# A feed-forward product as seven block products instead of eight, with its activations kept in DRAM

## The chip, the cores and the metric

The kernel runs on one core of a Trainium2 chip. The metric is the device time of one execution in microseconds (us); less is better. Before the change three runs gave 2440.69, 2441.7 and 2443.47 us, median 2441.7.

## The reference

One layer of a streaming encoder on 1024 tokens of 1024 channels, all float32. Four token mixers feed four gated branches that are merged and projected; what the change touches comes behind that:

```python
x = layer_norm(ALPHA * x + merged @ w_out[l], ln1_g[l], ln1_b[l])
ff = jnp.square(jax.nn.relu(x @ w_ff1[l])) @ w_ff2[l]          # 1024 -> 4096 -> 1024
ple = (p[l] @ w_ple[l]) * jax.nn.sigmoid(x @ w_ple_gate[l] + b_ple_gate[l])
x = layer_norm(ALPHA * x + ff + ple, ln2_g[l], ln2_b[l])
```

`p` has 256 channels. `ALPHA` is 2 to the power 1/4.

## The kernel before, in words

Every product of float32 operands is made from float32r parts: `Gemm.split` (L346) lets ScalarE copy a tile into its high part and VectorE subtract that to get the low part, and `Gemm.acc` (L362) issues three matmuls for each pair of 128x128 weights and 128x512 data: high by high (L367), high by low (L368), low by high (L369). `Gemm.load` (L350) brings a weight tile (512 KB for 1024 columns) into one of two buffers `wf` and splits it by halves into `wh` and `wl`, of which there are three each.

The program has four stretches: the mixers, attention along with the gates, the branches with the output projection `wo` and the first norm, and the feed-forward with the embedding. A scheduling layer sets the order on each engine from its own costs; within an engine instructions run in that order. Only the last stretch (L910 to L1072) changes.

- `norm` (L926) gives token-major tiles `x1[i]` of 128 tokens. `x1_transposed` (L948) turns a tile by eight TensorE transposes into PSUM (`tx`); ScalarE writes the high part `x1H` from there (L960) and VectorE the low part `x1L` (L961), channel-major.
- `feed_forward` (L1028) takes two of the 32 tiles of 128 hidden channels at a time (the last call four). For each tile and each half of the tokens (512) it needs 8 x 3 = 24 matmuls over the 1024 input channels (L1038), then relu on ScalarE (L1040), the square on GpSimd (L1041) and a split into `ah`, `al` in SBUF (L1042). The second product (L1057) follows at once: 16 half tiles of 128 tokens by 512 channels, 6 matmuls each (12 in the last call), added into `x1` by VectorE (L1061). The weights `w2f` are split at L1050.
- `embedding` (L991) runs twice, for 512 output channels each, token-major: 8 x 24 matmuls for the gate (`pg`, L1018), 8 x 6 for `p @ w_ple` (`pl`, L1024), then VectorE, ScalarE (tanh) and GpSimd (the sum into `x1`, L1026).
- The last call of `feed_forward` runs the second norm after each tile of tokens and stores it.

All DMAs are issued from SyncE's queue, in its order. `tmp` gives one of four 128x512 buffers; `pst` (L987) goes round all eight PSUM banks.

Of the kernel before, what the change touches and what calls it, by code (L numbers as in the profile page):

```python
# [45 lines left out]
class Rwkv:  # L46
    """RWKV-7 in chunks of 64 tokens; a unit is two chunks (128 tokens) of four heads.

    With D the decay accumulated within a chunk, at = -kk D[t-1], rt = r D[t], bt = kk a / D, kt = k / D, for kk
    before its normalisation, and g = 1 / |kk|^2 (token by token, on a diagonal):  # L50
    S = g (I - Aab g)^-1 (at P + Aak V), o = rt P + Qrb S + Qrk V, P' = D[end] (P + bt^T S + kt^T V).
    b and k are stacked on the partitions, (b|k) in a unit's first chunk and (k|b) in its second.
    """
# [34 lines left out]
    def unit(s, hf, b):  # L88
# [173 lines left out]
        # ---- the chunks in sequence  # L262
# [27 lines left out]
        # ---- group norm, bonus, gate  # L290
# [42 lines left out]
NG = 14        # gate tiles computed ahead, along with the recurrence  # L333
NH = 8         # gate tiles computed ahead, along with the attention
NA = 1.6       # attention steps traced per half tile of products around them


class Gemm:
    """Products of float32 operands, each split exactly into two float32r parts."""
# [10 lines left out]
    def load(s, dram, n, name, whole=False):  # L350
        """the k-tiles of a weight tile: [(hi, lo)]"""
# [21 lines left out]
def trunk(ctx, tc, xT, xn, pT, w_in, w_gate, w_branch, w_out, w_ff1, w_ff2, w_ple, w_pg,  # L373
          pvd, mud, bgd, lrud, lora, biasd, b256, rows, cstd, mskd, out):
# [48 lines left out]
    with tc.tile_pool(name="mx", bufs=1) as mx:  # L423
# [7 lines left out]
        for _ in range(NZ):   # the array's clock rises with use  # L431
            T.matmul(pz, wz[:, 0:128], wz, start=True, stop=True)
# [715 lines left out]
```

## Time and profile before

| what | value |
|---|---|
| median of three runs | 2441.7 us |
| span of the profiled execution | 2437.5 us, that is 4.2 us less than the median |
| TensorE busy | 2405.2 us, 99% |
| VectorE busy | 1217.1 us, 50% |
| ScalarE busy | 772.2 us, 32% |
| GpSimd busy | 222.5 us, 9% |
| memory traffic | 199.29 MB, mean 82 GB/s |
| stretch of the change | from about 1616 us, the end of `wo`, to the end |

The span is what the profile shows of one execution, and its own time isn't listed apart from it; the 4.2 us to the median stand for what lies around it. In the profile a matmul's duration covers its way through the array, and the next begins before it ends, so durations of matmuls overlap.

### The profile page before, as it was taken

What the parts mean: (1) busy time and instruction counts of PE and PEld (TensorE: products, weight loads), DVE (VectorE), ACT (ScalarE), POOL (GpSimd) and SP (SyncE); (2) the same over time, 40 slices, a digit from 0 to 9 for tenths busy, and PEclk for the clock granted to TensorE, in tenths of its full rate; (3) what the DMA queues carried; (4) which work ended last, traced back from release to release, by engine and by line L of the source; (5) the groups of instructions that cost most, each with busy time, mean ns of one, the idle gap of its engine ahead of it and who ended that gap; (6) DMA issues with size and microseconds to landing.
All of it is one profiled execution on the core that took longest, in us unless ns stands there. A gap on an engine that the chain in (4) does not pass through costs nothing.

```text
span 2437.5 us, 31399 instructions
## 1 busy us (share of the span) xinstructions
PE 2405.2 (99%) x12290; PEld 1984.6 (81%) x12290; DVE 1217.1 (50%) x2615; ACT 772.2 (32%) x1392; POOL 222.5 (9%) x238
## 2 busy tenths in 40 slices
PE   9999999999999999999999999999999999999998
PEld 7888787877777788878888887878888888888887
DVE  5354545767767542254534335664433434334337
ACT  5543323433424222243434343231212122121220
POOL 0000100010000100002111000001111010010111
PEclk9999999999999999999999999999999999999999
DMA  5531222121121112344412225321211111111112
GB/s 198 201 114 70 87 73 66 59 65 55 55 70 52 63 68 76 124 159 133 128 63 70 87 74 179 123 89 44 67 44 52 52 44 61 35 52 53 44 42 79
DMA packets 114563, 199.29 MB, mean 82 GB/s; under 512 B 18544, under 2 KB 53488, under 8 KB 114416
## 3 DMA queue, kind: packets, MB, share of 16 engines
q1 hardware_dynamic: 114416, 197.30, 24.6%
q8 instruction: 96, 1.57, 0.3%
q14 instruction: 51, 0.42, 0.1%
HBM read 154.27 MB, written 42.99 MB: 81 GB/s over the span
## 4 chain that ended last, share of the span: by engine, by line
PE 93%; DMA 2%; DVE 2%; ACT 1%; issue 1%; SPq 0%; POOL 0%; DVEq 0%; ACTq 0%; POOLq 0%
PE f L367 9%; PE f L369 9%; PE f L368 9%; PE ggt L368 4%; PE ggt L369 4%; PE ggt L367 4%; PE br L367 2%; PE br L369 2%; PE br L368 2%; PE gc L367 2%; PE gc L369 2%; PE gc L368 2%; PE gd L367 2%; PE gd L368 2%; PE po L785 2%; PE gd L369 2%
## 5 line engine op out<-in xcount | busy, mean ns | idle before, releaser
L369 PE MATMUL ggt<-xh,wlgt 128*128 128x512 f32 x512 | 202.5, 396 | 0.0
L367 PE MATMUL ggt<-xh,whgt 128*128 128x512 f32 x512 | 202.4, 395 | 0.0
L368 PE MATMUL ggt<-xl,whgt 128*128 128x512 f32 x512 | 202.1, 395 | 0.0
L367 PE MATMUL f<-w2h,ah 128*128 128x512 f32 x512 | 199.3, 389 | 0.9 <-ACT ah L347 0.9
L367 PE MATMUL f<-x1H,whf 128*128 128x512 f32 x512 | 199.3, 390 | 0.6 <-ACT x1H L960 0.6
L368 PE MATMUL f<-w2l,ah 128*128 128x512 f32 x512 | 199.2, 389 | 0.0
L368 PE MATMUL f<-x1L,whf 128*128 128x512 f32 x512 | 199.1, 389 | 0.0
L369 PE MATMUL f<-x1H,wlf 128*128 128x512 f32 x512 | 198.9, 389 | 0.0
L369 PE MATMUL f<-w2h,al 128*128 128x512 f32 x512 | 196.1, 389 | 0.0
L1061 DVE TENSOR_TENSOR x<-x,f 128x512 f32<-128x512 f32 x224 | 148.4, 685 | 73.3 <-PE f L369 72.6
L348 DVE TENSOR_TENSOR al<-rl,ah 128x512 fp32r<-128x512 f32 x64 | 44.2, 691 | 181.4 <-ACT ah L347 181.4
L1040 ACT ACTIVATE rl<-f 128x512 f32<-128x512 f32 x64 | 37.8, 591 | 272.5 <-PE f L369 272.5
L1041 POOL TENSOR_TENSOR rl<-rl 128x512 f32<-128x512 f32 x64 | 68.7, 1073 | 543.4 <-ACT rl L1040 543.4
L367 PEld LDWEIGHTS f<-w2h,ah 128*128 128x128 f32 x512 | 96.1, 188 | 21.1 <-ACT ah L347 1.2
L367 PEld LDWEIGHTS f<-x1H,whf 128*128 128x128 f32 x512 | 96.1, 188 | 20.8 <-ACT x1H L960 0.9
L368 PEld LDWEIGHTS f<-w2l,ah 128*128 128x128 f32 x512 | 96.1, 188 | 19.9
L369 PEld LDWEIGHTS f<-w2h,al 128*128 128x128 f32 x512 | 96.1, 188 | 20.0
L369 PEld LDWEIGHTS f<-x1H,wlf 128*128 128x128 f32 x512 | 96.1, 188 | 20.0
L368 PEld LDWEIGHTS f<-x1L,whf 128*128 128x128 f32 x512 | 96.1, 188 | 19.9
L369 PEld LDWEIGHTS ggt<-xh,wlgt 128*128 128x128 f32 x512 | 96.3, 188 | 19.1 <-issue 0.5
L368 PEld LDWEIGHTS ggt<-xl,whgt 128*128 128x128 f32 x512 | 96.3, 188 | 19.0 <-issue 0.3
L367 PEld LDWEIGHTS ggt<-xh,whgt 128*128 128x128 f32 x512 | 96.2, 188 | 18.3
(350 smaller groups left out, 5340.9 us busy)
## 6 DMA issues: line engine op xcount, KB each, us to landing
wfgt<-w_gate SPq DMA_DIRECT2D x32, 512.0 KB, 3.3
wff<-w_ff SPq DMA_DIRECT2D x32, 512.0 KB, 3.3
w2f<-w_ff SPq DMA_DIRECT2D x32, 512.0 KB, 3.3
gsd<-tg SPq DMA_DIRECT2D x44, 256.0 KB, 2.0
tl<-gsd SPq DMA_DIRECT2D x44, 256.0 KB, 3.1
zt<-zs SPq DMA_DIRECT2D x16, 640.0 KB, 5.0
qk<-qkv SPq DMA_DIRECT2D x64, 128.0 KB, 2.8
wfwb<-w_branch SPq DMA_DIRECT2D x32, 256.0 KB, 2.8
```

Source lines behind the costliest of these rows:

```text
L348: s.nc.vector.tensor_tensor(lo, src, hi.bitcast(F32), op=ALU.subtract)
L367: mm(ps, lh, rh, start=first and i == 0, stop=False)
L368: mm(ps, lh, rl, start=False, stop=False)
L369: mm(ps, ll, rh, start=False, stop=last and i == n - 1)
L785: T.matmul(po[:, 0:64], PT[:, c * 128:c * 128 + 128], vt[:, (k0 + c) * 128 + par * 64:(k0 + c) * 128 + par * 64 + 64], start=c == 0, stop= ...
L1040: A.activation(t, p, AF.Relu)
L1041: G.tensor_tensor(t, t, t, op=ALU.mult)
L1061: V.tensor_tensor(x1[i][:, sl], x1[i][:, sl], p, op=ALU.add)
```

## The change

The first feed-forward product and the embedding's gate product are computed in blocks of two by two: the weights of two hidden tiles by two halves of the input channels (a11, a12, a21, a22), the data by halves of the channels and of the tokens (blocks 11, 12, 21, 22). In place of eight block products of 12 matmuls, seven are made (Strassen's scheme in Winograd's form), from sums and differences of blocks.

- `combine` makes the sums of the data once, before the embedding: T1 = 12 - 11, T2 = 22 - T1, T3 = 22 - 12, T4 = 21 - T2, and splits 11, 21, T1, T2, T3, 22 and T4 into high and low parts. That is 28 splits of 128x512 and 16 subtractions of that size, those for T1 and T2 on VectorE, those for T3 and T4 on GpSimd. `x1_transposed` now only copies (`x1R`).
- `seven` does one pair of weight tiles: GpSimd makes S1 = a21 + a22, S2 = S1 - a11, S3 = a11 - a21 and S4 = a12 - S2, the last two in place in the `wf` buffers; each of the seven weight blocks is split, and the products accumulate in three PSUM banks a, b, c that are read between products.
- The embedding runs channel-major, four calls of `seven` (`pg0` to `pg3`), its bias now per partition in the tanh; each of its 16 results is turned back to tokens by four TensorE transposes (`pq`) and added to `x1` by four VectorE instructions of 128x128.
- All 16 calls of `seven` for the first product (`f10` to `f115`) come before the second product. Activations go to a DRAM tile `actd` as float32, 64 stores of 256 KB, and come back as 32 loads of 512 KB in `feed2`, where VectorE and ScalarE split them (`a2h`, `a2l`). The second product's matmuls are as before.

Its core:

```diff
+        def seven(w0, w1, name, sink, tiles=htmp):
+            wf = []
+            for i, w in enumerate((w0, w1)):
+                t = wp.tile([128, 1024], F32, tag="wf", name=f"wf{name}{i}", bufs=2)
+                SY.dma_start(t, w)
+                wf.append(t)
+            a11, a12, a21, a22 = (t[:, h * 512:h * 512 + 512] for t in wf for h in range(2))
+            def product(src, n, p, x, first=True):
+                wh = wp.tile([128, 512], F32R, tag="wh", name=f"wh{name}{n}")
+                wl = wp.tile([128, 512], F32R, tag="wl", name=f"wl{name}{n}")
+                gm.split(src, wh, wl)
+                gm.acc(p, [(wh[:, k * 128:k * 128 + 128], wl[:, k * 128:k * 128 + 128]) + XB[x, k] for k in range(4)], first, skip_group_check=not first)
...
+            a = ps("g", f"a{name}")
+            product(a11, 1, a, "11")
+            p1 = tiles(f"p1{name}")
+            A.activation(p1, a, AF.Copy)
+            c = ps(f"r{ns[0] % 2}", f"c{name}")
+            product(a12, 2, c, "21")
+            V.tensor_tensor(p1, c, p1, op=ALU.add)
+            sink(0, 0, p1, None)
+            yield
+            s1 = total(1, a21, a22, ALU.add)
+            s2 = total(2, s1, a11, ALU.subtract)
+            product(s2, 3, a, "T2", first=False)
+            u2 = tiles(f"u2{name}")
+            A.activation(u2, a, AF.Copy)
+            b = ps("q", f"b{name}")
+            product(s1, 4, b, "T1")
+            p5 = tiles(f"p5{name}")
+            A.activation(p5, b, AF.Copy)
+            s3, s4 = a21, a12
+            G.tensor_tensor(s3, a11, a21, op=ALU.subtract)
+            G.tensor_tensor(s4, a12, s2, op=ALU.subtract)
+            product(s3, 5, a, "T3", first=False)
+            V.tensor_tensor(p5, a, p5, op=ALU.add)
+            sink(1, 1, p5, None)
+            product(s4, 6, b, "22", False)
+            V.tensor_tensor(u2, b, u2, op=ALU.add)
+            sink(0, 1, u2, None)
+            product(a22, 7, a, "T4", False)
+            sink(1, 0, None, a)
...
+                p3 = ps("s", f"pq{ct}{j}")
+                for q in range(4):
+                    T.transpose(p3[:, q * 128:q * 128 + 128], t[:, q * 128:q * 128 + 128], ident)
+                for q in range(4):
+                    xs_ = x1[4 * j + q][:, ct * 128:ct * 128 + 128]
+                    V.scalar_tensor_tensor(xs_, xs_, ALPHA, p3[:, q * 128:q * 128 + 128], op0=ALU.mult, op1=ALU.add)
...
+        def feed1(n):
+            def sink(i, j, t, p):
+                if t is None:
+                    t = htmp(f"rl{n}{i}{j}")
+                A.activation(t, t if p is None else p, AF.Relu)
+                G.tensor_tensor(t, t, t, op=ALU.mult)
+                SY.dma_start(actd[2 * n + i, :, j * 512:j * 512 + 512], t)
...
+        def feed2(n, fs, last=False):
             act, w2 = [], []
+            for f in fs:
+                for src, dst, nm in ((actd[f], act, "a"), (w_ff2[f], w2, "w")):
+                    wf = wp.tile([128, 1024], F32, tag="wf", name=f"{nm}2f{f}", bufs=2)
+                    SY.dma_start(wf, src)
+                    hi, lo = place(f"{nm}2h{f}"), place(f"{nm}2l{f}")
+                    gm.split(wf, hi, lo)
+                    dst.append((hi, lo))
```

How the order moves, at three places. First VectorE, between the last transposes of `x1` (`tx70`, `tx71`) and the first block products. Before, its rows there were short low parts of `x1`, straight from PSUM, and the first feed-forward weights and activations:

```order
L939 SCALAR_TENSOR_TENSOR x1_7_14317<-xr70_14260,mvn17_14319,b1_13687 128x512
L939 SCALAR_TENSOR_TENSOR x1_7_14317<-xr71_14289,mvn17_14319,b1_13687 128x512
L961 TENSOR_TENSOR x1L31_14352<-tx41_14342,x1H31_14351 128x2x128
L961 TENSOR_TENSOR x1L21_14348<-tx51_14364,x1H21_14347 128x2x128
L961 TENSOR_TENSOR x1L11_14339<-tx50_14355,x1H11_14338 128x2x128
L348 TENSOR_TENSOR pg00_14697<-pgf00_14695,pg00_14697 128x512
L348 TENSOR_TENSOR pg10_14700<-pgf00_14695,pg10_14700 128x512
L961 TENSOR_TENSOR x1L01_14335<-tx60_14373,x1H01_14334 128x2x128
```

Now, behind the copies of the last two transposes, stand the sums and splits of all blocks (`xT2l0` is the low part of T2):

```order
L971 TENSOR_SCALAR x1R01_14330<-tx70_14371 128x2x128
L971 TENSOR_SCALAR x1R21_14339<-tx71_14378 128x2x128
L1026 TENSOR_TENSOR x1R00_14048<-x1R01_14330,x1R00_14048 128x512 x2
L1026 TENSOR_TENSOR x1R10_14050<-x1R11_14332,x1R10_14050 128x512 x2
L1031 TENSOR_TENSOR xT20_14401<-x1R21_14339,x1R00_14048 128x512
L348 TENSOR_TENSOR x22l0_14448<-x1R21_14339,x22h0_14447 128x512
L1031 TENSOR_TENSOR xT20_14401<-x1R21_14339,x1R00_14048 128x512
L348 TENSOR_TENSOR x22l0_14448<-x1R21_14339,x22h0_14447 128x512
L1031 TENSOR_TENSOR xT21_14410<-x1R31_14341,x1R10_14050 128x512
L348 TENSOR_TENSOR x22l2_14454<-x1R31_14341,x22h2_14453 128x512
L1031 TENSOR_TENSOR xT21_14410<-x1R31_14341,x1R10_14050 128x512
```

From the copy of `tx71` to the split of the seventh weight block (`wlpg07`) VectorE has 32 such full-width rows, one of 1024 columns and one TENSOR_SCALAR.

Second, GpSimd in the middle of the first product. Before, it had only the squares:

```order
L1041 TENSOR_TENSOR rl150_17296<-rl150_17296 128x512
L1041 TENSOR_TENSOR rl151_17326<-rl151_17326 128x512
L1041 TENSOR_TENSOR rl160_17508<-rl160_17508 128x512
L1041 TENSOR_TENSOR rl161_17538<-rl161_17538 128x512
L1041 TENSOR_TENSOR rl170_17580<-rl170_17580 128x512
```

Now the sums of the next pair of weights stand between the squares of this one (`f19` is one call of `seven`, `f110` the next):

```order
L1142 TENSOR_TENSOR p1f19_16695<-p1f19_16695 128x512
L1074 TENSOR_TENSOR S1f110_16865<-wff1101_16823 128x512
L1142 TENSOR_TENSOR p5f19_16757<-p5f19_16757 128x512
L1074 TENSOR_TENSOR S2f110_16867<-S1f110_16865,wff1100_16821 128x512
L1097 TENSOR_TENSOR wff1101_16823<-wff1100_16821,wff1101_16823 128x512
L1142 TENSOR_TENSOR u2f19_16738<-u2f19_16738 128x512
L1098 TENSOR_TENSOR wff1100_16821<-wff1100_16821,S2f110_16867 128x512
L1142 TENSOR_TENSOR rl910_16817<-rl910_16817 128x512
```

There are eight instructions of GpSimd for each call, four of them sums that the next call's weight blocks wait for.

Third, VectorE at the begin of the second product, which now stands by itself:

```order
L348 TENSOR_TENSOR a2l4_18014<-a2f4_18011,a2h4_18013 128x1024
L1183 TENSOR_TENSOR x1_7_14313<-x1_7_14313,f2070_17843 128x512
L348 TENSOR_TENSOR w2l4_18020<-w2f4_18017,w2h4_18019 128x1024
L1183 TENSOR_TENSOR x1_7_14313<-x1_7_14313,f2071_17851 128x512
L1183 TENSOR_TENSOR x1_0_13751<-x1_0_13751,f2100_17883 128x512
L1183 TENSOR_TENSOR x1_0_13751<-x1_0_13751,f2101_17891 128x512
L348 TENSOR_TENSOR a2l5_18026<-a2f5_18023,a2h5_18025 128x1024
L1183 TENSOR_TENSOR x1_1_13821<-x1_1_13821,f2110_17899 128x512
```

Splits of loads that are needed a group later stand between the sums that free the PSUM banks (`f2070` and so on). On TensorE everything up to the output projection stands in the old order.

## Rows read from the trace of the kernel before

**Rows 1.** The page, busy time by engine: us, share of the span, instructions.
```profile
span 2437.5 us, 31399 instructions
...
PE 2405.2 (99%) x12290; PEld 1984.6 (81%) x12290; DVE 1217.1 (50%) x2615; ACT 772.2 (32%) x1392; POOL 222.5 (9%) x238
```

**Rows 2.** The page, costliest groups: count, busy us, mean ns, idle before.
```profile
L369 PE MATMUL f<-x1H,wlf 128*128 128x512 f32 x512 | 198.9, 389 | 0.0
```

**Rows 3.** Timeline of TensorE in the feed-forward: start, us; 19 rows of matmuls between.
```profile
1900.33 0.39 PE L367 MATMUL f<-w2h,ah 128*128 128x512 f32 x1
...
1904.86 0.39 PE L369 MATMUL f<-w2h,al 128*128 128x512 f32 x1
```

**Rows 4.** Windows: length, busy us of PE, PEld, DVE, ACT, POOL; PE clock, DMA.
```profile
1620.00:1630.00 10.00, 7.60 (x40) 5.62 (x39) 9.73 (x22) 5.53 (x16) 2.67 (x2) 1.00 0.55 207
1900.00:1950.00 50.00, 50.00 (x223) 41.38 (x222) 21.39 (x31) 9.26 (x14) 4.20 (x4) 1.00 0.13 43
```

**Rows 5.** Timeline of TensorE around four transposes of the norm's result.
```profile
1596.56 0.60 PE L954 MATMUL tx<-ident,x 128*128 128x128 f32 x4
1596.91 0.48 PE L367 MATMUL wo<-woh,mH 128*128 128x512 f32 x1
1597.23 0.40 PE L368 MATMUL wo<-wol,mH 128*128 128x512 f32 x1
```

**Rows 6.** Groups by form on VectorE, 1630 to 2390 us.
```profile
L1061 DVE TENSOR_TENSOR x<-x,f 128x512 f32<-128x512 f32 x209 | 138.1, 685 | 71.7 <-PE f L369 71.5
...
L348 DVE TENSOR_TENSOR wlf<-wff,whf 128x512 fp32r<-128x512 f32 x61 | 42.0, 692 | 61.4 <-ACT whf L347 60.2
L348 DVE TENSOR_TENSOR w2l<-w2f,w2h 128x1024 fp32r<-128x1024 f32 x30 | 36.8, 1226 | 45.3 <-ACT w2h L347 45.3
...
L1022 DVE TENSOR_SCALAR pt<-pt 128x512 f32<-128x512 f32 x16 | 6.8, 426 | 8.7 <-ACT pt L1021 8.7
```

**Rows 7.** Groups by form, evacuation of transposes by VectorE, 1560 to 1660 us.
```profile
L961 DVE TENSOR_TENSOR x1L<-tx,x1H 128x256 fp32r<-128x256 f32 x32 | 11.9, 416 | 0.9 <-ACT x1H L960 0.9
```

**Rows 8.** Groups by form on ScalarE, 1630 to 2390 us.
```profile
L347 ACT ACTIVATE whf<-wff 128x512 fp32r<-128x512 f32 x61 | 38.5, 634 | 63.5 <-PE f L368 54.2 <-DMA wff<-w_ff 6.7
...
L347 ACT ACTIVATE w2h<-w2f 128x1024 fp32r<-128x1024 f32 x30 | 31.9, 1063 | 85.6 <-DMA w2f<-w_ff 73.8 <-PE pl L369 11.8
```

**Rows 9.** Groups by form on GpSimd, 1630 to 2390 us.
```profile
L1041 POOL TENSOR_TENSOR rl<-rl 128x512 f32<-128x512 f32 x63 | 66.9, 1062 | 539.4 <-ACT rl L1040 539.4
L1026 POOL TENSOR_TENSOR x<-x,pt 128x512 f32<-128x512 f32 x16 | 20.6, 1288 | 132.5 <-DVE pt L1025 132.5
```

**Rows 10.** Timeline of VectorE and GpSimd at the last transposes of the first norm.
```profile
1625.46 1.29 DVE L348 TENSOR_TENSOR pg<-pgf,pg 128x512 fp32r<-128x512 f32 x2
...
1625.90 1.75 POOL L1041 TENSOR_TENSOR rl<-rl 128x512 f32<-128x512 f32 x1 [3.92 <-ACT rl L1040]
```

**Rows 11.** Windows at two places where TensorE's granted clock fell.
```profile
295.00:300.00 5.00, 2.70 (x18) 2.14 (x18) 2.67 (x10) 1.23 (x3) 0.00 (x0) 1.00 0.47 133
300.00:305.00 5.00, 4.41 (x21) 3.95 (x22) 2.61 (x6) 0.61 (x2) 0.00 (x0) 0.73 0.01 3
305.00:310.00 5.00, 5.00 (x29) 3.85 (x27) 0.00 (x0) 0.60 (x1) 0.00 (x0) 0.93 0.00 0
...
845.00:850.00 5.00, 5.00 (x22) 4.49 (x22) 3.06 (x10) 1.20 (x2) 0.00 (x0) 0.51 0.00 0
850.00:855.00 5.00, 4.78 (x26) 4.21 (x25) 1.38 (x2) 0.60 (x1) 0.00 (x0) 0.81 0.00 0
```

**Rows 12.** The page, DMA issues: count, KB each, us to landing.
```profile
wff<-w_ff SPq DMA_DIRECT2D x32, 512.0 KB, 3.3
...
gsd<-tg SPq DMA_DIRECT2D x44, 256.0 KB, 2.0
```

**Rows 13.** Timeline, the last matmul and the end of VectorE's last norm.
```profile
2428.46 0.39 PE L369 MATMUL f<-w2h,al 128*128 128x512 f32 x1
...
2433.17 1.41 DVE L939 SCALAR_TENSOR_TENSOR x<-x,mvn,b2r 128x512 f32<-128x512 f32 x2
```

More of the change, by code (lines that the diff above doesn't have):

```diff
@@ L360, in load, with acc @@
         return r
-    def acc(s, ps, terms, first=True, last=True):
+    def acc(s, ps, terms, first=True, last=True, **kw):
         n = len(terms)
@@ new lines, in places, with two, combine @@
+        def places():
+            for k in range(8):
+                yield "s1", k
+                yield "s2", k
+            for k in range(4):
+                yield "s3", 2 * k + 1
+                yield "s5", 2 * k + 1
+        pl = places()
+        def two():
+            return next(pl), next(pl)
+        def combine():
+            for kp in range(2):
+                block("21", 2 * kp, raw[2 + kp, 0], two())
+            for kp in range(2):
+                for c in range(2):
+                    V.tensor_tensor(raw[kp, 0][:, c, :], raw[kp, 1][:, c, :], raw[kp, 0][:, c, :], op=ALU.subtract)
+            t2 = []
+            for kp in range(2):
+                t2.append(slot("s3", 8 + kp, [128, 2, 512], F32, f"xT2{kp}"))
+                for c in range(2):
+                    V.tensor_tensor(t2[kp][:, c, :], raw[2 + kp, 1][:, c, :], raw[kp, 0][:, c, :], op=ALU.subtract)
+                block("T2", 2 * kp, t2[kp], two())
+            for kp in range(2):
+                block("T1", 2 * kp, raw[kp, 0], two())
+            for kp in range(2):
+                for c in range(2):
+                    G.tensor_tensor(raw[kp, 1][:, c, :], raw[2 + kp, 1][:, c, :], raw[kp, 1][:, c, :], op=ALU.subtract)
+                block("T3", 2 * kp, raw[kp, 1], two())
+            for kp in range(2):
+                block("22", 2 * kp, raw[2 + kp, 1], two())
+            for kp in range(2):
+                for c in range(2):
+                    G.tensor_tensor(raw[2 + kp, 0][:, c, :], raw[2 + kp, 0][:, c, :], t2[kp][:, c, :], op=ALU.subtract)
+                block("T4", 2 * kp, raw[2 + kp, 0], two())
@@ new lines, in embedding, with run_all, sink @@
+            plw = pools["s5"].tile([128, 2, 2, 256], F32R, tag="plw", name=f"plw{n}")
+            gm.split(wf, plw[:, 0], plw[:, 1])
+            yield from seven(w_pg[2 * n], w_pg[2 * n + 1], f"pg{n}", sink, tmp)
+        def run_all(it):
+            for _ in it:
+                pass
+        def feed1(n):
+            def sink(i, j, t, p):
+                if t is None:
+                    t = htmp(f"rl{n}{i}{j}")
+                A.activation(t, t if p is None else p, AF.Relu)
+                G.tensor_tensor(t, t, t, op=ALU.mult)
+                SY.dma_start(actd[2 * n + i, :, j * 512:j * 512 + 512], t)
+            yield from seven(w_ff1[2 * n], w_ff1[2 * n + 1], f"f1{n}", sink)
@@ new lines, in trunk @@
+        combine()
+        pTh, pTl = [], []
+        for k in range(2):
+            pf = slot("s6", 2 * k, [128, 1024], F32, f"pf{k}")
+            SY.dma_start(pf, pT[k])
+            pTh.append(slot("s6", 2 * k + 1, [128, 1024], F32R, f"ph{k}"))
+            pTl.append(slot("s5", 4 * k, [128, 1024], F32R, f"pl{k}"))
+            gm.split(pf, pTh[k], pTl[k])
+        es_ = [embedding(n) for n in range(4)]
+        fs_ = [feed1(n) for n in range(16)]
+        for f in es_ + fs_:
+            run_all(f)
@@ L1118, in _pack @@
     d['b256'] = f(g['rel_bias'][:, 256])
-    d['rows'] = np.stack([g['ln1_g'][0], g['ln1_b'][0], g['ln2_g'][0], g['ln2_b'][0], g['b_ple_gate'][0]])
+    d['rows'] = np.stack([g['ln1_g'][0], g['ln1_b'][0], g['ln2_g'][0], g['ln2_b'][0]])
     d['cstd'] = consts_np()
```

151 lines of the change are left out of this document (64 added, 87 removed).

## Prediction

> **What bounds the kernel now.** I read the busy times first: TensorE is busy 99% of the span, VectorE 50%, GpSimd 9% [rows 1]. In the feed-forward a window of 50 us has TensorE busy for all of it, VectorE for 21.39 us and GpSimd for 4.20 us, at a granted clock of 1.00 [rows 4]. So this stretch lasts as long as its matmuls take, and a matmul less is time less.
>
> What a matmul takes must be read from starts, not durations. The group's mean is 389 ns [rows 2], but from 1900.33 to 1904.86 us there are twenty steps from start to start, (1904.86 - 1900.33) / 20 = 0.2265 us [rows 3]. The durations overlap. Check: the stretch has 3072 feed-forward and 480 embedding matmuls, 3552 x 0.2265 = 804.5 us, and from the end of `wo` near 1616 us to the last matmul's start at 2428.46 us [rows 13] there are some 812 us, with 2.4 us of idle time [rows 4] and a few transposes in it. Behind the last matmul comes VectorE's norm to about 2434.6 us [rows 13]; that tail stays.
>
> **Removed.** The first product goes from 1536 to 16 x 84 = 1344 matmuls, the gate from 384 to 4 x 84 = 336. `p @ w_ple` keeps 96, the second product 1536. That is 192 + 48 = 240 fewer, all on the path: 240 x 0.2265 = **-54.4 us**.
>
> **Added on TensorE.** 16 groups of four transposes turn the embedding back. Four transposes and one matmul took 1597.23 - 1596.56 = 0.67 us [rows 5]; less one matmul of 0.2265 that is 0.44 us. 16 x 0.44 = **+7.1 us**. The bounds are 0.35 us (the next start, 1596.91 - 1596.56) and 0.6 us (their recorded duration): 5.6 to 9.6 us. VectorE's 64 short additions from PSUM are bounded by 0.42 us, what 128x256 took [rows 7], above and by nothing below; VectorE has room for either between block products.
>
> **The start of the feed-forward.** Before, the norm's transposes needed only short low parts, and TensorE lost 10.00 - 7.60 = 2.4 us [rows 4]. Now the sums of blocks must be formed from all eight token tiles. From the copies of the last transposes to the seventh weight block VectorE's order has 2 evacuations, 32 full-width instructions, one of 1024 columns and one TENSOR_SCALAR: 2 x 0.416 [rows 7] + 32 x 0.69 + 1.23 + 0.43 [rows 6] = 24.6 us. ScalarE's high parts run a step ahead at 0.634 us each [rows 8]. In that time TensorE has products 1, 3, 4, 5, 6 of the first call and six matmuls of `pl`, 66 x 0.2265 = 14.9 us. So it waits 24.6 - 14.9 = 9.7 us. There is less cover for the last norm, too: of the first call's products only product 2 stands ahead of the last transposes, and product 1 (12 x 0.2265 = 2.7 us), which was ready, comes behind them. I count that as a further loss of 3 us. Together **+12.7 us**. The lower end is 3, if VectorE's list were worked through while TensorE is still in `wo`; the upper some 20, if ScalarE's high parts or GpSimd's sums held VectorE's list up for another 7 us.
>
> GpSimd makes T3 and T4 beside this, eight subtractions with two inputs at 1.29 us [rows 9], 10.3 us, or 14 us at the 1.75 us of the one that ran beside two VectorE splits [rows 10]. Both are below 24.6, so they stay hidden.
>
> **The clock after the wait.** After 2.3 us of idle time within five the granted clock of the next windows was 0.73 and 0.93, and at 845 us, in windows that were busy, 0.51 and 0.81 [rows 11]: that is, some of each at the lower level, 1.2 GHz. In lost time, 5 x (0.27 + 0.07) = 1.7 us and 5 x (0.49 + 0.19) = 3.4 us. The start now has longer waits than either, so I take **+3 us**, between 0 (the 2.4 us of idle time now leave the clock at 1.00 [rows 4]) and 5 (two falls of the mean size). The Trainium skill, "TensorE: Matmul & The Clock Gate", section "HAM oscillation — how this bites in real kernels", says that waits between bursts send the array back to its low clock and that the bursts behind them then run cold; by that rule the fall is certain and comes again with each wait. The trace agrees at 295 us and not at 1620 us [rows 4, 11]; by that rule the sum would hold the upper end, 5, and give 2414.
>
> **The steady part.** A call of `seven` is 84 x 0.2265 = 19.0 us, a block product 2.72 us. Beside it, for one call:
> - VectorE: seven splits and three sums, 10 x 0.69 = 6.9 us [rows 6]. ScalarE: seven high parts, three copies, four relus, 14 x 0.63 = 8.8 us [rows 8]. GpSimd: four sums at 1.29 and four squares at 1.06 [rows 9], 9.4 us. All under half.
> - Waits: there are three `wh` buffers, so the split for product n starts when product n-3 ends; it takes 0.63 + 0.69 = 1.3 us, and two products (5.4 us) cover it. The PSUM reads between products (first a high part, then a copy, 1.3 us after the product) have 2.7 us until the bank is written again.
> - The weights: both `wf` buffers belong to one call. The second is free when product 7's weights are split, some 1.4 us after product 4; then 3.3 us to land [rows 12], two GpSimd sums (2.6 us) and a split (1.3 us): 8.6 us. The next call's product 3 needs it five products (13.6 us) after product 4. Slack 5.0 us; for the first buffer, by the same count, over 4 us.
> - SyncE: the stores of activations stand ahead of the next loads, but each waits only for a square that is ready a product earlier. 1 MB loaded and 1 MB stored in 19.0 us is 110 GB/s, where the trace had 207 GB/s over 10 us [rows 4].
>
> I cost it at **nothing**. If a cover were gone, the price is 20 times the wait.
>
> **The second product.** VectorE per group of 96 matmuls (21.7 us): 16 sums at 0.685 and four splits at 1.226 [rows 6], 15.9 us, 73%. At the hand-over the first loads wait for `wf` of the last call, so the chain landing 3.3, high part 1.06, low part 1.23 [rows 6, 8, 12] ends about when product 7 does. Later, splits of future groups stand between the sums that free PSUM: a pair of loads takes 5.6 us, four half tiles 5.4 us; eight banks (10.9 us) absorb the difference. I take **+2 us**, between 0 and 6.
>
> **Sum.** -54.4 + 7.1 + 12.7 + 3 + 2 = -29.6 us. On the profiled execution 2437.5 - 29.6 = 2407.9; with the 4.2 us by which the median stands above that span, **2412 us**. The terms' ends together would give 2396 to 2428; since they hardly all fall on one side, this case's own range is 2400 to 2424.
>
> **The rivals.** About 5 us, 0.2%, is what a measurement of this kernel tells from no change.
> - *The start is nearly free* (13%). The scheduler may have spread the sums so that only 3 us are added and the clock holds: 2441.7 - 54.4 + 7.1 + 3 = 2397. For it: ScalarE and GpSimd are free there. Against it: VectorE was busy 9.73 of 10 us in that window already [rows 4].
> - *GpSimd and VectorE block each other* (8%). The eight subtractions of GpSimd hold VectorE up one by one: 8 x 1.29 = 10.3 us more at the start, 2422. Against it: where both ran, GpSimd's instruction grew to 1.75 us, while VectorE's pair took 1.29 us, twice its usual 0.69 less overlap [rows 10]. The Trainium skill, "SBUF — State Buffer", speaks of a shared port pair held for a whole instruction while the loser fully blocks. By that rule either side can lose; the trace shows it for GpSimd alone.
> - *A small bubble in every call* (11%). A late evacuation or sum costs TensorE 1 us in each of 20 calls: 2432. For it: the slack behind PSUM reads is only 1.4 us. Against: each engine is under half busy.
> - *Slower: the weights don't arrive in time* (4%). With both `wf` buffers in one call, a landing that lies open in each call costs 20 x 3.3 = 66 us: 2478. It decides from 29.6 / 20 = 1.5 us per call. Against it stands the slack of 4 to 5 us.
>
> **Chances.** The forecast has 62%, the rivals 13, 8, 11 and 4, and 2 are left for the unforeseen. Faster by over 0.2% means below 2436.8: 62 + 13 + 8 + 11 = 94%, less a little for larger bubbles, 0.93; slower 0.04; same 0.03. The range takes the first three cases and part of the fourth: 2396 to 2431.
>
> **What would show it.** In the profile after: matmul starts 0.2265 us apart; 50 us windows full between about 1665 us and the end; in the window of the start some 12 us of TensorE idle time put down to VectorE's and ScalarE's block parts, with a clock below 1.00; a call each 19.0 us; GpSimd near 50%. I am wrong if idle time repeats every 19 us, if the second product's windows show TensorE waiting for VectorE's sums, or if the start takes no longer than now.

## The result and the profile after

| | before | changed |
|---|---|---|
| median of the runs | 2441.69 us (2440.69 to 2443.47, 4 runs) | 2411.45 us (2409.42 to 2414.82, 4 runs) |
| ratio | | 0.9882, 95% interval 0.9865 to 0.9899 |
| span of the profiled execution | 2437.5 us | 2413.0 us (2414.82 us, the slowest of the four) |

The forecast was 2412 us, 2396 to 2431. Busy times after, to be held against [rows 1]:

```profile
span 2413.0 us, 31988 instructions
...
PE 2369.2 (98%) x12114; PEld 1951.1 (81%) x12114; DVE 1353.1 (56%) x2758; ACT 845.9 (35%) x1478; POOL 345.2 (14%) x310
```

TensorE lost 36 us of busy time, VectorE gained 136. Three windows of the changed kernel (length; busy us of PE, PEld, DVE, ACT, POOL with instruction counts; clock; DMA): the gate, the first product, the second.

```profile
1680.00:1730.00 50.00, 50.00 (x234) 41.12 (x233) 32.30 (x65) 17.63 (x28) 11.29 (x8) 1.00 0.13 43
1800.00:2000.00 200.00, 200.00 (x884) 165.58 (x884) 91.11 (x106) 87.09 (x148) 111.60 (x86) 1.00 0.30 110
2100.00:2300.00 200.00, 200.00 (x880) 164.75 (x879) 145.08 (x192) 42.61 (x42) 0.00 (x0) 1.00 0.34 109
```

As in [rows 4], TensorE is full; in the first product it takes 200 / 884 = 0.2262 us a matmul. In these windows GpSimd reaches 56% and VectorE 73%. The profile records no wait of TensorE from 1662 us to its last matmul, so no idle time returns every 19 us. The start does not look so; the same columns, 1620 to 1660 us:

```profile
1620.00:1625.00 5.00, 4.48 (x30) 3.61 (x29) 5.00 (x12) 3.23 (x8) 0.51 (x1) 1.00 0.00 2
1625.00:1630.00 5.00, 1.74 (x7) 0.89 (x5) 5.00 (x9) 2.81 (x6) 5.00 (x1) 0.87 0.00 0
1630.00:1635.00 5.00, 0.00 (x0) 0.00 (x0) 3.19 (x6) 1.07 (x3) 5.00 (x2) 0.50 0.28 105
1635.00:1640.00 5.00, 3.35 (x8) 2.68 (x9) 5.00 (x5) 4.72 (x10) 5.00 (x4) 0.50 0.00 0
1640.00:1645.00 5.00, 3.84 (x12) 2.48 (x10) 5.00 (x4) 1.90 (x3) 5.00 (x4) 0.76 0.00 0
1645.00:1650.00 5.00, 2.61 (x7) 1.82 (x6) 5.00 (x9) 2.71 (x4) 0.26 (x1) 0.58 0.06 11
1650.00:1655.00 5.00, 4.22 (x11) 2.99 (x10) 2.70 (x5) 2.66 (x4) 0.00 (x0) 0.50 0.57 212
1655.00:1660.00 5.00, 5.00 (x21) 4.01 (x20) 3.42 (x4) 1.68 (x3) 2.38 (x2) 0.90 0.23 92
```

40 - 25.24 = 14.8 us idle, and a granted clock below 1.00 in every window from 1625 to 1660 us, down to 0.50 (the lower level, 1.2 GHz), where before there were 2.4 us of idle time at 1.00 [rows 4]. At that level matmuls start 0.42 or 0.43 us apart:

```profile
1638.10 0.63 PE L367 MATMUL bpg<-xT1h,whpg 128*128 128x512 f32 x1
1638.52 0.63 PE L368 MATMUL bpg<-xT1l,whpg 128*128 128x512 f32 x1
1638.95 0.63 PE L369 MATMUL bpg<-xT1h,wlpg 128*128 128x512 f32 x1
```

TensorE's longest waits there (waiter, releaser; us in total, times, longest; `apg` and `bpg` are the banks a and b of the gate's calls, `xT2h` and `xT2l` the high and low part of T2, `ph` the high part of `p`):

```profile
PE apg L367 <- ACT xT2h L347: 9.3, 1, 9.3
PE pl L367 <- ACT ph L347: 2.4, 1, 2.4
PE apg L368 <- DVE xT2l L348: 1.2, 1, 1.2
```

The timeline of the other engines (start, us, engine, line, operation; in brackets the idle time before and what ended it) shows why T2's high part is late:

```profile
1624.49 14.01 POOL L1037 TENSOR_TENSOR x1R<-x1R,x1R 128x512 f32<-128x512 f32 x4 [4.59 <-DVE x1R L1026]
...
1633.93 0.63 ACT L347 ACTIVATE xT3h<-x1R 128x512 fp32r<-128x512 f32 x1 [6.12 <-POOL x1R L1037]
...
1634.59 1.08 DVE L348 TENSOR_TENSOR xT3l<-x1R,xT3h 128x512 fp32r<-128x512 f32 x1 [1.81 <-ACT xT3h L347]
...
1635.98 0.62 ACT L347 ACTIVATE xT2h<-xT 128x512 fp32r<-128x512 f32 x1
```

and those of VectorE by themselves, and GpSimd's four subtractions for T3 (ns min/median/max):

```profile
1626.07 0.69 DVE L1031 TENSOR_TENSOR xT<-x1R,x1R 128x512 f32<-128x512 f32 x1
1626.67 0.69 DVE L348 TENSOR_TENSOR x22l<-x1R,x22h 128x512 fp32r<-128x512 f32 x1
...
1640.66 1.76 DVE L348 TENSOR_TENSOR xT3l<-x1R,xT3h 128x512 fp32r<-128x512 f32 x1
1642.35 1.76 DVE L348 TENSOR_TENSOR xT2l<-xT,xT2h 128x512 fp32r<-128x512 f32 x1
...
1651.41 1.28 DVE L348 TENSOR_TENSOR wlpg<-wfpg,whpg 128x512 fp32r<-128x512 f32 x2
```

```profile
L1037 POOL TENSOR_TENSOR x1R<-x1R,x1R x4: 1263/1728/9405, 1624.5 to 1636.8; 128x512 f32<-128x512 f32 x4
```

GpSimd's first subtraction begins at 1624.49, when the T1 subtraction that it waited for has ended, and ends 9.4 us later, at 1633.90. Until 1632.8 VectorE runs instructions with two tensors from SBUF back to back, one each 0.60 us (1626.07, 1626.67), not slowed. GpSimd gets through only when VectorE runs dry then. The scheduler had put T3's first high part ahead of T2's on ScalarE, which goes in order: it waited 6.12 us, VectorE 1.81 us for it, TensorE 9.3 us. From there to 1645 us the two engines alternate: most subtractions take 1.73 us and most low parts 1.76, starts 1.69 apart where they were 0.60.

**One measure for all kernels.** The first matmul of `wo` starts anywhere from 1509.4 to 1518.4 us in the profiles of this study, though TensorE's order ahead of it is the same: the changed kernel alone has 1514.5, and 1518.4 when run again (e4). That is scatter between executions. So the kernels are also compared by the stretch from the first `wo` matmul to the last of the second product. Before, and after:

```profile
L367 PE MATMUL wo<-woh,mH x128: 389/389/477, 1514.7 to 1615.6; 128*128 128x512 f32 x128
...
L369 PE MATMUL f<-w2h,al x512: 388/389/389, 1631.7 to 2428.5; 128*128 128x512 f32 x171
```

```profile
L367 PE MATMUL wo<-woh,mH x128: 387/389/477, 1514.5 to 1615.4; 128*128 128x512 f32 x128
...
L367 PE MATMUL f<-w2h,a2h x512: 387/389/496, 2053.5 to 2403.2; 128*128 128x512 f32 x171
...
L369 PE MATMUL f<-w2h,a2l x512: 387/389/398, 2055.1 to 2403.7; 128*128 128x512 f32 x171
```

2428.5 - 1514.7 = 913.8 us before, 2403.7 - 1514.5 = 889.2 after: 24.6 less. The other kernels, with the same two rows read:

| kernel | median us | ratio to before on the same chip | stretch us |
|---|---|---|---|
| changed | 2411.45 | 0.9882 (0.9865 to 0.9899) | 889.2 |
| e4, the same again | 2413.73 | 0.9888 (0.9867 to 0.9908) | 889.3 |
| e1, eight products | 2449.41 | 1.0043 (1.0026 to 1.0059) | 925.1 |
| e8, e1 with unread GpSimd work | 2452.65 | 1.0050 (1.0032 to 1.0068) | 926.0 |
| e2, subtractions on VectorE | 2403.30 | 0.9860 (0.9839 to 0.9882) | 880.0 |
| e12, T3's alone on VectorE | 2410.74 | 0.9872 (0.9855 to 0.9890) | 885.3 |
| e5, T3 from T2 | 2409.74 | 0.9872 (0.9852 to 0.9893) | 886.9 |
| e3, fillers | 2411.83 | 0.9891 (0.9872 to 0.9910) | 887.0 |
| e9, e2 and fillers | 2405.53 | 0.9861 (0.9843 to 0.9878) | 880.2 |
| e6, e2 and earlier transposes | 2407.36 | 0.9858 (0.9838 to 0.9878) | 882.3 |
| e7, e6 by token tile | 2409.86 | 0.9870 (0.9849 to 0.9891) | 883.9 |
| e10, e6 and order of TensorE | 2407.95 | 0.9868 (0.9850 to 0.9887) | 882.8 |
| e11, sums on VectorE | 2412.08 | 0.9882 (0.9866 to 0.9898) | 889.3 |

The intervals of most ratios overlap; the stretch is one profile each, and its two readings of the changed kernel differ by 0.1 us. Differences of 1 or 2 us between two stretches thus rest on one execution of each.

### The profile page after: what moved, and what is told of

Its sections match the earlier page's. It is cut to its first block, busy times and chain, and to the rows that moved or that the text cites. A ratio compares the mean times of both kernels' runs of the same rounds, so it can differ in the third digit from the quotient of the medians.

```text
span 2413.0 us, 31988 instructions
## 1 busy us (share of the span) xinstructions
PE 2369.2 (98%) x12114; PEld 1951.1 (81%) x12114; DVE 1353.1 (56%) x2758; ACT 845.9 (35%) x1478; POOL 345.2 (14%) x310
## 4 chain that ended last, share of the span: by engine, by line
PE 91%; DVE 3%; DMA 3%; ACT 1%; issue 1%; POOL 0%; SPq 0%; DVEq 0%; ACTq 0%; POOLq 0%
PE f L368 5%; PE f L367 5%; PE f L369 5%; PE ggt L368 4%; PE ggt L369 4%; PE ggt L367 4%; PE af L369 2%; PE af L368 2%; PE af L367 2%; PE gc L368 2%; PE gc L369 2%; PE gc L367 2%; PE br L369 2%; PE br L367 2%; PE br L368 2%; PE gd L367 2%
## 5 line engine op out<-in xcount | busy, mean ns | idle before, releaser
L368 PE MATMUL f<-w2l,a2h 128*128 128x512 f32 x512 | 200.0, 391 | 0.0
L369 PE MATMUL f<-w2h,a2l 128*128 128x512 f32 x512 | 199.7, 390 | 0.0
L367 PE MATMUL f<-w2h,a2h 128*128 128x512 f32 x512 | 198.0, 390 | 0.0
L367 PEld LDWEIGHTS f<-w2h,a2h 128*128 128x128 f32 x512 | 96.0, 188 | 21.0 <-ACT w2h L347 0.3
L368 PEld LDWEIGHTS f<-w2l,a2h 128*128 128x128 f32 x512 | 96.1, 188 | 20.6
L369 PEld LDWEIGHTS f<-w2h,a2l 128*128 128x128 f32 x512 | 96.1, 188 | 20.6
L367 PE MATMUL br<-yh,whwb 128*128 128x512 f32 x256 | 101.8, 398 | 3.2 <-ACT tg L413 1.8
L369 PE MATMUL br<-yh,wlwb 128*128 128x512 f32 x256 | 101.5, 396 | 0.1
L368 PE MATMUL br<-yl,whwb 128*128 128x512 f32 x256 | 100.9, 394 | 0.0
L369 PE MATMUL gc<-xh,wlc 128*128 128x512 f32 x224 | 88.1, 394 | 0.0
```

What stands on the lines that cost most here:

```text
L367: mm(ps, lh, rh, start=first and i == 0, stop=False, **kw)
L368: mm(ps, lh, rl, start=False, stop=False, **kw)
L369: mm(ps, ll, rh, start=False, stop=last and i == n - 1, **kw)
```

## The experiments

**e1: eight products.** The products alone are undone.

```diff
-    product(a11, 1, a, "11")
...
-    product(a22, 7, a, "T4", False)
-    sink(1, 0, None, a)
+    for i, (u, v) in enumerate(((a11, a12), (a21, a22))):
...
+        for j in range(2):
+            p = ps((("g", r), ("q", "g"))[i][j], f"p{name}{i}{j}")
+            gm.acc(p, [(wh[n][:, k * 128:k * 128 + 128], wl[n][:, k * 128:k * 128 + 128]) + XB[f"{n + 1}{j + 1}", k] for n in range(2) for k in range(4)])
+            sink(i, j, None, p)
```

> Undoes the seven products alone: each call makes eight block products again (12 matmuls each), without sums of blocks; the pass through DRAM, the channel-major embedding and its transposes stay. If the seven products are worth 240 x 0.2265 us less what the longer start costs, this comes out at 2411.5 + 54.4 minus the lost start (12 to 19 us) = 2447 to 2454 us, that is 5 to 12 us above the kernel before: the price of transposes and of the second product from DRAM. The start then has no sums and should lose some 2 to 5 us as in the kernel before. Rival: calls of seven hold a hidden loss of their own, as a bubble in each; then this comes out lower, at 2441 or below.

2449.41 us, and the stretch is 11.3 us longer than before. So what e1 keeps of the change (the pass through DRAM, the channel-major gate with its transposes, the splits of evacuated blocks) costs 11.3 us, and the seven products give 925.1 - 889.2 = 35.9: 54.4 for the matmuls less 18.5, which by the full windows above lies in the start. It is what the changed kernel's start loses beyond e1's: TensorE of e1 waits 2.9 us there, 2.5 of them for the last norm.

**e2: the subtractions for T3 and T4 on VectorE.**

```diff
-    G.tensor_tensor(raw[kp, 1][:, c, :], raw[2 + kp, 1][:, c, :], raw[kp, 1][:, c, :], op=ALU.subtract)
+    V.tensor_tensor(raw[kp, 1][:, c, :], raw[2 + kp, 1][:, c, :], raw[kp, 1][:, c, :], op=ALU.subtract)
...
-    G.tensor_tensor(raw[2 + kp, 0][:, c, :], raw[2 + kp, 0][:, c, :], t2[kp][:, c, :], op=ALU.subtract)
+    V.tensor_tensor(raw[2 + kp, 0][:, c, :], raw[2 + kp, 0][:, c, :], t2[kp][:, c, :], op=ALU.subtract)
```

> The eight subtractions for T3 and T4 go from GpSimd to VectorE. Theory of the prediction (the start lasts as long as VectorE's list): the list grows by 8 x 0.69 = 5.5 us, the time to 2411.5 + 5.5 = 2417 us. Rival (the start lasts as it does because GpSimd's first subtraction takes 9.4 us beside VectorE's two-input instructions, and ScalarE, in order, waits 6.1 us for it with T2's high parts behind): that wait is gone and VectorE's splits take 0.69 us in place of 1.75; TensorE's wait of 9.3 us for T2 shrinks by 4 us or more: 2402 to 2408 us.

2403.3 us; the stretch is 9.2 us shorter, though VectorE has eight instructions more. The theory that the start lasts as long as VectorE's count of instructions, whatever runs beside it, has fallen. The low parts are back at 0.68 us; TensorE's longest waits and two windows of this kernel:

```profile
PE bpg L368 <- DVE xT1l L348: 3.9, 1, 3.9
PE apg L367 <- ACT xT2h L347: 2.6, 1, 2.6
```

```profile
1620.00:1630.00 10.00, 2.89 (x9) 1.53 (x8) 10.00 (x17) 9.04 (x18) 0.00 (x0) 0.67 0.00 1
1630.00:1640.00 10.00, 9.02 (x32) 6.85 (x32) 10.00 (x18) 5.25 (x9) 0.00 (x0) 0.82 0.15 52
```

VectorE is busy for all of it, so most of what is left of the loss is put down to its list, which now goes at one instruction each 0.60 us.

**e3: fillers.** 36 matmuls into the bank that T1's product overwrites, in the first call.

```diff
+    b = ps("q", f"b{name}")
+    if fill and ns[0] == 1:
+        for _ in range(fill):
+            T.matmul(b, XB["11", 0][0][:, 0:128], XB["11", 0][0], start=True, stop=True)
```

> 36 matmuls whose result is overwritten stand between product 1 and the products of T1 and T2 in the first call alone, 36 x 0.2265 = 8.2 us in TensorE's wait of 9.3 us; the other engines keep their order. If the fall of the clock behind that wait costs time (matmuls 0.43 us apart from 1637 to 1642 and from 1647 to 1656 us in the profile of the changed kernel), the granted clock stays at 1.00 there and the time falls by 3 to 6.5 us: 2405 to 2408 us. Rival: behind the wait TensorE goes at the pace of the block parts anyway, and the clock only fills waits: no change, 2411 us. If the wait is shorter in other runs, the filler itself is in the way, by at most 8.2 us: 2419.

No change in the time, 2.2 us in the stretch. One window of the changed kernel and of this one:

```profile
1620.00:1660.00 40.00, 25.25 (x87) 18.47 (x86) 34.30 (x47) 20.77 (x38) 23.15 (x10) 0.70 0.14 53
```

```profile
1620.00:1660.00 40.00, 32.21 (x125) 24.70 (x126) 35.49 (x47) 21.91 (x40) 24.59 (x11) 0.91 0.15 53
```

The granted clock rose from 0.70 to 0.91, and little came of it: behind the wait TensorE goes mostly at the pace of the block parts, which the rival said.

**e4: the changed kernel again**, beside e5 to e7.

> The changed kernel as it is, so that the three kernels beside it are compared on the same chip and more of its runs are seen: 0.988 of the kernel before, as in the first comparison; its starts (from the last matmul of the output projection to the first of the second product) should lie near the 437.7 us of the first profile or up to 6 us below, where its clock falls for a shorter time.

Ratio 0.9888, stretch 889.3, with the same wait of 9.3 us. In its five runs the mean clock went from 0.994 at 2409.03 us to 0.989 at 2418.83.

**e5: T3 = T2 - x11**, so that ScalarE's high parts of T2 come first. (T1 is then formed in the place of block 12, not of 11.)

```diff
...
-    G.tensor_tensor(raw[kp, 1][:, c, :], raw[2 + kp, 1][:, c, :], raw[kp, 1][:, c, :], op=ALU.subtract)
+    G.tensor_tensor(raw[kp, 0][:, c, :], t2[kp][:, c, :], raw[kp, 0][:, c, :], op=ALU.subtract)
```

> T3 is formed from T2 (T3 = T2 minus the first block) in place of from two evacuated blocks, so GpSimd can't begin before T2 exists and ScalarE's high parts of T2 stand ahead of those of T3; GpSimd keeps its eight subtractions. If ScalarE's order is what costs (it waited 6.1 us for GpSimd's first T3 with T2's high parts behind it), this wins 3 to 6 us over the changed kernel: ratio to the kernel before 0.9858 to 0.987. If the cost is that VectorE's splits take 1.75 us in place of 0.69 while GpSimd subtracts (8 subtractions of some 1.73 us, 13.9 us long), the stretch is only moved: no change from the changed kernel, 0.988.

2.3 us in the stretch, less than the 3 to 6 for the order alone and more than nothing. The wait for T2's high parts fell from 9.3 to 2.6 us, and this came in its place:

```profile
PE apg L368 <- DVE xT2l L348: 5.5, 3, 2.4
```

GpSimd's first subtraction still took 7.6 us and the others 1.7. The low parts of T2 are late here because VectorE's low parts beside GpSimd start 1.69 us apart, as in the changed kernel. But ScalarE, too, still waited 4.19 us for that first subtraction, with two of T2's four high parts behind it. So e5 shows that the order isn't all of the cost; how the 9.2 us of e2 divide between the order and the slowing stays open.

What let GpSimd through is to be seen here as well, for VectorE had no pause:

```profile
1624.09 7.62 POOL L1037 TENSOR_TENSOR x1R<-xT,x1R 128x512 f32<-128x512 f32 x1 [7.00 <-ACT xT1h L347]
```

```profile
1631.74 0.63 ACT L347 ACTIVATE xT3h<-x1R 128x512 fp32r<-128x512 f32 x1 [4.19 <-POOL x1R L1037]
```

```profile
1630.48 0.69 DVE L1084 TENSOR_TENSOR p1pg<-cpg,p1pg 128x512 f32<-128x512 f32 x1
1631.08 1.18 DVE L348 TENSOR_TENSOR xT1l<-x1R,xT1h 128x512 fp32r<-128x512 f32 x1
```

The instruction at 1630.48 takes one of its operands from PSUM (`cpg`). From its start to the end of GpSimd's subtraction at 1631.71 are 1.23 us, about the 1.26 of the shortest one; the low part behind it was the first that was slowed.

**e6: e2 with earlier transposes.**

```diff
-    for t in {4: (0,), 5: (1, 2), 6: (3,)}.get(i, ()):
+    for t in {3: (0,), 4: (1, 2), 5: (3,), 6: (4, 5)}.get(i, ()):
         x1_transposed(t)
-    if i == 6:
+    if i == 5:
...
-    for i in range(4, 8):
+    for i in range(6, 8):
```

> On top of the eight subtractions on VectorE: the token tiles are transposed one to two tiles earlier, inside the loop over tiles (tiles 4 and 5 ahead of the last two), so the first block's splits and four of VectorE's evacuations leave the stretch behind the output projection, and T1's low parts come ahead of T2's subtractions on VectorE. If the start is now as long as VectorE's list behind the output projection (it was busy for all of 1610 to 1645 us there), TensorE's wait of 3.9 us for T1's low parts goes and 3 to 6 us are won over the kernel with the subtractions on VectorE: ratio 0.9835 to 0.9848. Rival: the wait only moves to T2 and T3, whose parts need the last tile: under 2 us, 0.9852 to 0.986.

Nothing over e2: 882.3 against 880.0 us. The wait for T1's low parts fell to 1.7 us, but 3.5 us for T2's and 3.0 us for `p`'s high part (a load that waits for T1's place) came instead. The rival held.

**e7: e6 with T1 and T3 by token tile.**

```diff
...
+    if hh:
+        for kp in range(2):
+            if kq == 0:
+                V.tensor_tensor(raw[kp, 0][:, :, cs], raw[kp, 1][:, :, cs], raw[kp, 0][:, :, cs], op=ALU.subtract)
+            else:
+                V.tensor_tensor(raw[kp, 1][:, :, cs], raw[2 + kp, 1][:, :, cs], raw[kp, 1][:, :, cs], op=ALU.subtract)
```

> On top of the earlier transposes: the subtractions for T1 and T3 are made per token tile, 16 of 256 columns in place of 8 of 512, right after each tile's evacuation; half of them come before the last two tiles. VectorE has 8 x 0.68 = 5.4 us less and 8 x some 0.4 = 3.2 us more behind the output projection: 2 us won over the kernel with the earlier transposes, if its list sets the start. Rival: VectorE is full before the end of the output projection too (10.00 of 10 us from 1600 us on), so the evacuations and norms come later and nothing is won, or up to 2 us are lost.

883.9 us, 1.6 more than e6; again the rival. TensorE now waited 2.5 us for the last norm, where e6 has 0.7; that the extra instructions hold it up is likely, not shown.

**e8: GpSimd work that nobody waits for**, in e1.

```diff
+    scr = slot("s3", 8, [128, 512], F32, "scr")
+    for _ in range(8):
+        G.tensor_tensor(scr, x1[6][:, 0:512], x1[7][:, 512:1024], op=ALU.subtract)
```

> The kernel with eight block products, with eight GpSimd subtractions of 128x512 added at its start whose result nobody reads (from the last two token tiles into a free tile, right behind the last norm). Nothing waits for them, so if GpSimd costs time only through those that wait for its results, this takes as long as without them: 925.1 us from the first matmul of the output projection to the last of the second product. If GpSimd and VectorE slow each other where both read two tensors from SBUF, the eight subtractions take some 1.7 us each in place of 1.29, VectorE's low parts beside them 1.75 in place of 0.69, and the start gets 2 to 8 us longer.

Three low parts of VectorE in e1, the same three in e8, and GpSimd's eight:

```profile
1624.82 1.89 DVE L348 TENSOR_TENSOR x12l<-x1R,x12h 128x512 fp32r<-128x512 f32 x3 [0.97 <-ACT x12h L347]
```

```profile
1625.87 4.67 DVE L348 TENSOR_TENSOR x12l<-x1R,x12h 128x512 fp32r<-128x512 f32 x3 [0.97 <-ACT x12h L347]
```

```profile
L1116 POOL TENSOR_TENSOR scr<-x,x x8: 1274/1616/2154, 1623.9 to 1635.7; 128x512 f32<-128x512 f32 x8
```

The slowing stands alone here: 1.89 us became 4.67 with no data shared. The starving does not show: none of these eight took more than 2154 ns. GpSimd's first began at 1623.9, when VectorE had none of its two-operand instructions under way. The time is a miss, 0.9 us in the stretch where 2 to 8 were expected: TensorE had other products ready and waited only 0.7 us for a low part, that of `p`.

**e9: e2 with 24 fillers**, the edits of e2 and e3 together.

> The eight subtractions on VectorE, and 24 matmuls whose result is overwritten ahead of the products of T1 and T2 in the first call, which keep TensorE at work for 5.4 us of its wait. With the subtractions on VectorE alone 12 matmuls after the wait ran 0.43 us apart, 2.4 us lost; the fillers keep the clock at 1.00 there: 1 to 2.5 us less than the 880.0 us from the first matmul of the output projection to the last of the second product (889.2 in the changed kernel). Rival: what follows waits for VectorE's low parts and nothing is won: 880.

880.2 us against 880.0. The clock never fell:

```profile
1620.00:1630.00 10.00, 9.48 (x43) 7.47 (x42) 10.00 (x19) 9.45 (x21) 0.00 (x0) 1.00 0.00 1
1630.00:1640.00 10.00, 6.39 (x24) 3.94 (x23) 10.00 (x18) 4.53 (x8) 0.00 (x0) 1.00 0.15 52
1640.00:1650.00 10.00, 8.28 (x36) 6.46 (x36) 10.00 (x16) 6.27 (x11) 0.52 (x1) 1.00 0.43 159
```

and TensorE waits later instead, with VectorE at 10.00 of 10. The rival held: in this kernel, where VectorE's list sets the end of the start, keeping the clock up was worth nothing.

**e10: e6 with `p @ w_ple` behind T1's product and 16 fillers.**

```diff
-    sink(0, 0, p1, None)
+    late = ns[0] == 1
+    if not late:
+        sink(0, 0, p1, None)
...
     product(s1, 4, b, "T1")
+    if late:
+        pz = ps("s", "fill")
+        for _ in range(fill):
+            T.matmul(pz, XB["T1", 0][0][:, 0:128], XB["T1", 3][0], start=True, stop=True)
+        sink(0, 0, p1, None)
```

> The earlier transposes with the subtractions on VectorE, and two edits on TensorE's order in the first call: the six matmuls of p @ w_ple, for whose operand TensorE waited 3.0 us there, come behind T1's product, with 16 matmuls whose result is not used ahead of T2's. If the earlier transposes did not win since TensorE's order met a late operand and the clock then fell for 13.7 us, this falls below both the 882.3 us of the earlier transposes and the 880.0 us of the subtractions on VectorE alone: 876 to 879. Rival: VectorE's list still sets the end of the start: 880 to 882.

882.8 us: a miss. The edit did not take the wait for `p` away (still 2.3 us) nor keep the clock up all through, so it says little on what earlier transposes could give. That stays open.

**e11: the sums of weight blocks on VectorE**, from the second call on.

```diff
-    G.tensor_tensor(t, u, v, op=op)
+    (G if ns[0] == 1 else V).tensor_tensor(t, u, v, op=op)
```

> The changed kernel with the four sums of weight blocks of every call but the first on VectorE in place of GpSimd, 19 x 4 instructions. The prediction counted the steady calls as free of waits; VectorE then has 6.9 + 4 x 0.69 = 9.7 us of work in a call of 19.0 us: no change in the first product (313.5 us from its first matmul to the second product's), 889 us over the whole stretch, although GpSimd and VectorE no longer meet there. If a part of each call was lost by their meeting, 19 times that part comes back; a loss of 0.2 us in each would be 4 us.

889.3 us, no change. The low parts of the first product's weights, in the changed kernel and here:

```profile
L348 DVE TENSOR_TENSOR wlf<-wff,whf x80: 681/692/1721, 1737.0 to 2046.0; 128x512 fp32r<-128x512 f32 x80
```

```profile
L348 DVE TENSOR_TENSOR wlf<-wff,whf x80: 675/684/693, 1735.0 to 2043.3; 128x512 fp32r<-128x512 f32 x80
```

The two engines do meet in the changed kernel's steady calls (up to 1721 ns) and the slack covers it, as the prediction had it.

**e12: T3's four subtractions alone on VectorE**, the first edit of e2.

> Only the four subtractions for T3 go to VectorE; those for T4 stay on GpSimd, and ScalarE's order now has T4's high parts between those of T2. If the price is paid by the instruction, as two engines that read the same memory (a split of VectorE starts 1.69 us after the last beside GpSimd, 0.60 us alone: some 1.1 us lost by each of GpSimd's subtractions, 0.60 us for one on VectorE), four of them give half of the 9.2 us: 884 to 885 us from the first matmul of the output projection to the last of the second product. If it was the order alone (T3 stood ahead of T2 on ScalarE), all of it comes back here unless T4 takes T3's place ahead of T2: then TensorE's wait for T2's high parts stays near 9 us, and the stretch near 889.

885.3 us, 0.3 above the 884 to 885 of a price by the instruction. The waits show a mixture, so the near hit doesn't prove that price: GpSimd's first subtraction, now for T4, is the one starved (max 10037 ns), and ScalarE waited 6.60 us for it, but T2's first high part had gone ahead. It ended 1.23 us after VectorE began the same instruction with an operand in PSUM as in e5 (1635.86 us).

```profile
L1043 POOL TENSOR_TENSOR x1R<-x1R,xT x4: 1722/1740/10037, 1627.1 to 1640.4; 128x512 f32<-128x512 f32 x4
```

```profile
1635.86 0.68 DVE L1084 TENSOR_TENSOR p1pg<-cpg,p1pg 128x512 f32<-128x512 f32 x1
```

## Why the prediction was right, point by point

- **What bounds, and the matmuls removed: right.** The first product goes at 0.2262 us a matmul where 0.2265 were taken, and its windows are full.
- **Transposes: right.** Four in the gate of the changed kernel, with one matmul behind:

```profile
1703.99 0.40 PE L369 MATMUL apg<-xT2h,wlpg 128*128 128x512 f32 x1
1704.22 0.60 PE L1122 MATMUL pq<-ident,u2pg 128*128 128x128 f32 x4
1704.58 0.48 PE L367 MATMUL pl<-ph,plw 128*128 128x512 f32 x1
1704.89 0.39 PE L368 MATMUL pl<-pl,plw 128*128 128x512 f32 x1
```

1704.89 - 1704.22 = 0.67 us, to the hundredth what [rows 5] gave.
- **The steady calls at nothing: right**, by the full windows, e1 and e11.
- **The second product, +2: right in size, not in cause.** From 2053.5 to 2403.7 us its 1535 steps take 350.2 us, at 0.2265 they would take 347.7: 2.5 us. No wait for VectorE's sums is to be seen: the windows are full, yet hold 880 matmuls in 200 us where the first product has 884; some 45 steps in them are 0.24 us long, in the first product none. Why is open.
- **The start, +12.7, and the clock, +3: mis-sized, and the step that failed is the cover of GpSimd's subtractions.** The stretch leaves 54.4 - 24.6 - 7.1 - 2.5 = 20.2 us for both terms together, where 15.7 were counted (the 18.5 of e1 leave out what e1's own start loses). The prediction compared GpSimd's 14 us with VectorE's 24.6 as if each went at its own pace. The eight subtractions did not stay hidden. VectorE's list, from the copy at 1621.40 us to the seventh weight block at 1652.69, took 31.3 us. Its 33 full-width instructions at 0.60, five copies at 0.33 and two others (1.13 and 0.34) make 22.9; the other 8.4 are 1.8 of waiting and 6.6 of instructions slowed beside GpSimd. That the prediction took 0.69 a step, a recorded duration, where starts lie 0.60 apart, hid part of this: the same error that it warns of for matmuls.
- **The rival of engines that block each other (8%, 10.3 us more at the start) had the mechanism that took place.** Its size did not come: the start was 4.5 us dearer than counted, and e2, with VectorE doing the subtractions, is 9.2 us shorter. Its total of 2422 did not come either. It was set low because the one instance in [rows 10] showed VectorE's pair unlengthened. The Trainium skill, "SBUF — State Buffer", section "SBUF: two separate sides", says that the pair of ports is held for a whole instruction by whichever starts first, and lists a VectorE instruction with two SBUF inputs against a GpSimd one that reads SBUF. The runs agree that both can lose (1.76 us and 1.73 us in turns), and that VectorE's instruction with an operand in PSUM held nothing up (e5). They differ on who comes first: the GpSimd instruction that began at 1624.49 us lost to thirteen later ones in a row.
- **The clock: it fell as counted, but less hung on it.** 26 matmuls in the start are 0.40 to 0.43 us apart, some 5 us more than at 0.2265; filling the longest wait gave back 2.2 us (e3), and nothing where VectorE's list was the limit (e9). The Trainium skill, "TensorE: Matmul & The Clock Gate", section "HAM oscillation — how this bites in real kernels", says that a wait between bursts throttles the array again and the next burst starts cold; the trace agrees, 0.50 behind the wait of 9.3 us. What the fall cost hung on whether operands were there.
- **That the total fell on 2412 is partly luck.** The sum had 29.6 us saved, and the medians differ by 30.2. But the stretch that the change touches is only 24.6 us shorter, 5 less than the sum, nearly all of it the dearer start. The rest of the 30.2 is which executions were profiled. The changed kernel's is the slowest of four, 3.4 us above their median; its time is 1.8 us above its span (2414.82 - 2413.0), and if that holds before, the profiled execution of before was 2.4 us faster than its median. How much of the 30.2 us between the medians is the change itself, and not scatter ahead of the stretch, one profile of before doesn't tell; e4, on another chip, has a like gap (29.2 in the medians, 24.5 in the stretch).

The best version found is e2, with the shortest stretch and an edit of two letters. Its ratio, 0.9860, is level with those of e6 (0.9858) and e9 (0.9861), which have the same subtractions on VectorE. It was timed on another chip than the changed kernel, each against the kernel before, and their intervals overlap by a little: that e2 is faster rests on the stretch.

## What to carry to other kernels

Before counting work on GpSimd as hidden, look whether VectorE runs instructions with two SBUF operands in that stretch: here the two engines then took turns, and a GpSimd result that another in-order engine awaited was late by thirteen VectorE instructions. Where VectorE itself is the bound, an element-wise subtraction may cost it less (0.60 us) than the same one on GpSimd beside it (1.69 - 0.60, about 1.1 us of VectorE's time). A wait that is filled, or a clock that is kept up, gives little (2.2 us in e3, nothing in e9) while the list behind it is the limit.

## What the runs showed of the hardware

- A GpSimd subtraction of 128x512, 1.26 us at its shortest, took 9.4, 7.6 and 10.0 us beside back-to-back VectorE instructions with two SBUF operands, which were not slowed (0.60 us apart). It got through when VectorE paused (changed kernel) or began an instruction with one operand in PSUM (e5, e12: 1.23 us from that start to its end). After that the two alternated, 1.73 and 1.76 us.
- The output projection begins anywhere from 1509.4 to 1518.4 us behind the same order of TensorE; one profile of each kernel can't be compared by its span to better than that.
- TensorE started 880 matmuls in 200 us of the second product and 884 in the first, at the same clock and with no idle time in either.
